# Rotary embedding by copies out of PSUM in place of a product with a permutation, and a forget gate with both weight parts in one tile, in a two-block transformer kernel on one Trainium2 core

## The chip, the cores and the metric

The kernel runs on one core of a Trainium2 chip. The metric is the device time of one launch in microseconds (us). Five engines matter: PE multiplies matrices (PEld is its weight load), DVE and ACT work elementwise, POOL does small sums, fills and a few transfers, and SP issues the large transfers. Each takes its instructions strictly in the order in which the program lists them. PE writes into PSUM, here eight banks of 128 partitions x 512 f32; DVE and ACT read it.

## The reference, cut to what matters

A sequence of 256 tokens of width 1024 goes through a first block (two mixers and a mixture of experts), then through two layers of a second block. Each of these two layers is: feed-forward, mixer, feed-forward. The change lies in the mixer alone, which therefore runs twice. There, eight "fox" heads have a forget gate, and four "diff" heads have a rotary embedding on q and k:

```
proj = h @ w_in
fq, fk, fv, ff, dq, dk, dv = jnp.split(proj, IN_OFFSETS, axis=-1)
log_f = jax.nn.log_sigmoid(ff + forget_bias);  cum_f = jnp.cumsum(log_f.transpose(0, 2, 1), axis=-1)
def _apply_rope(t, cos, sin):
    t1, t2 = jnp.split(t, 2, axis=-1)          # halves of a head of 64
    rot = jnp.concatenate([-t2, t1], axis=-1)
    return t * cos + rot * sin
```

All matrices are f32. A product is computed from parts: hi is the factor rounded for PE's fast f32r form and lo is the rest, and three products (hi hi, hi lo, lo hi) are summed in PSUM.

## The kernel before, in words

**Weights.** SP loads weights into slots. For each half of a slot (128x1024), ACT makes `whi` (L140) and DVE makes `wlo` (L154). The class Feeder holds six such pairs: a pair is refilled when PE is done with it, so `whi` waits for PE, and `wlo` waits for `whi`. The fill instructions stand in the queues of ACT and DVE among all their other work, at the place where the program called `fd.done` or `fd.tick`.

**Order in the mixer.** `feat_block` (L324) computes 512 columns of the projection, transposed (columns on partitions, tokens along the row), in two PSUM banks: eight steps of 12 matmuls each. After each step it calls `fd.tick`, which advances the background generators by one `yield`: this is what places the mixer's small work. Four PSUM buffers `g` go round, two for each block. The sequence is: dv (`skew_first`), dk, dq, fk, fq (four `feat_block`s), fv (`tok_block`), then the output product.

- `small_parts` (L1567) runs in the ticks of the dk block: `rsb` (the norm's row scales), the forget gate product `ff` (8 steps of three matmuls, L295 to L297), then the chain of small operations on `fz` and `fe` with Exp and Ln on ACT (L1581 to L1589), and last cos and sin times the row scales, `cr` and `sr` (L1594, L1595). WH and WL hold hi and lo of the gate weights in 128 columns of which 8 are used.
- `rope` (L1606) runs in the ticks of the block behind its own: for k in the dq block, for q in the fk block. ACT copies both banks to `raw` (L1610). After two ticks, for each bank b: PE multiplies `raw` by the permutation `rot` (L1616, plain f32), DVE multiplies this by `sr` (L1618) and `raw` by `cr` (L1619), and adds the two into the heads (L1627 for k, in two halves; L1630 for q).
- `diff` (L1640 on) starts when q is done: scores on PE (`ds`, L1648 and L1649), masked maximum on DVE (L1529, L1530), Exp on ACT (L1531, L1532), normalization on DVE (L1659 to L1665), transposes `t` (L1635) and the product with v (`do`). `ds` and `t` share two PSUM buffers `a`. `fox` follows in the same way.

Of the kernel before, what the change touches and what calls it, by code (L numbers as in the profile page):

```python
# [10 lines left out]
F32 = mybir.dt.float32  # L11
# [5 lines left out]
AF = mybir.ActivationFunctionType  # L17
ALU = mybir.AluOpType
# [8 lines left out]
NEG = -1e30  # L27
# [153 lines left out]
def body(tc, A, out, taps=None, stop=None):  # L181
# [3 lines left out]
    with es:  # L185
# [12 lines left out]
        def pa(name="a"):  # L198
            return psum.tile([128, 512], F32, tag="a", name=name, bufs=2)
# [7 lines left out]
        mm = nc.tensor.matmul  # L207
        act = nc.scalar.activation
        dve = nc.vector
        pool = nc.gpsimd  # L210
# [83 lines left out]
        def mm3(o, sh, sl, mh, ml, start, stop, skip=False):  # L294
            mm(o, sh, mh, start=start, stop=False, skip_group_check=skip)  # L295
            mm(o, sh, ml, start=False, stop=False, skip_group_check=skip)  # L296
            mm(o, sl, mh, start=False, stop=stop, skip_group_check=skip)  # L297
# [81 lines left out]
        XH, XL = halves(const, ("XH", "XL"))  # L379
# [97 lines left out]
        banks = feat_block()  # L477
        for h in range(4):
            z = halfbank(banks, h)
# [5 lines left out]
        banks = feat_block()  # L485
        for h in range(4):
            z = halfbank(banks, h)
# [4 lines left out]
        for i in range(2):  # L492
            c = slice(i * 512, (i + 1) * 512)
# [212 lines left out]
        banks = tok_block()  # L706
# [4 lines left out]
        banks = feat_block()  # L711
        for c in range(4):
            act(qm[:, c], halfbank(banks, c), AF.Identity, bias=qb8[:, c:c + 1], scale=-0.125)
        banks = feat_block()
        for c in range(4):
            z = halfbank(banks, c)
            act(kp[0:64, 2 * c], z[0:64], AF.Identity, bias=bcol[0:64, 20 + c:21 + c])
            act(kp[64:128, 2 * c + 1], z[64:128], AF.Identity, bias=bcol[64:128, 20 + c:21 + c])
        banks = tok_block()
# [614 lines left out]
        cos_, sin_ = aux[:, 0:256], aux[:, 256:512]  # L1334
        PTs = [aux[:, 1024 + i * 384:1408 + i * 384] for i in range(2)]
        wff = wr[:, 0:128].rearrange("p (l n) -> p l n", l=2)
        rot, tri = aux[:, 512:640], aux[:, 640:896]
        pool.dma_start(aux[:, 512:896], A["late"])

        def gain(row):  # L1340
            g = work.tile([128, 1024], F32, name="gain", bufs=1)
# [192 lines left out]
        def mixer(l, g_next):  # L1534
# [11 lines left out]
            PD = [s_p[:, i * 384:(i + 1) * 384] for i in range(5)]  # L1546
            PF = [xn[i // 2][:, (i % 2) * 384:(i % 2 + 1) * 384] for i in range(4)]
            WH = OH[:, 0:4].rearrange("p c (a n) -> p (c a) n", n=128)
            WL = OL[:, 0:4].rearrange("p c (a n) -> p (c a) n", n=128)
            wf = wff[:, l].rearrange("p (k n) -> p k n", k=8)  # L1550
            banks = [pg(), pg()]
            skew_first(banks)
            for a in (OH, OL):
                pool.memset(a[:, 0:4].bitcast(F32), 0.0)
            for a in (s_kd, s_qf, s_kf):
                pool.memset(a, 0.0)
            for a in (qf, kf):
                pool.memset(a[64:66, 0:8:2], 1.0)
                pool.memset(a[0:2, 1:8:2], 1.0)
            act(WH[:, :, 0:8], wf, AF.Copy)  # L1560
            dve.tensor_sub(WL[:, :, 0:8], wf, WH[:, :, 0:8].bitcast(F32))
            for t in range(2):
                act(vd[:, t], banks[t], AF.Copy, scale=RS[t][:, 0:1])

            def small_parts():
                yield from wait(2)
                rows = rstd_rows()  # L1567
                next(rows)
                yield from wait(3)
                for _ in rows:  # L1570
                    pass


                p = pa("ff")
                for k in range(8):
                    mm3(p[:, 0:256], WH[:, k], WL[:, k], XH[:, k], XL[:, k], k == 0, k == 7)
                    if k == 3:
                        yield
                z = work.tile([8, 256], F32, name="fz", tag="fh")
                e = work.tile([8, 256], F32, name="fe", tag="fh")  # L1580
                dve.tensor_tensor(z, p[0:8, 0:256], rsb[0:8], ALU.mult)  # L1581
                dve.tensor_scalar(z, z, fbi[:, l:l + 1], None, op0=ALU.add)
                dve.scalar_tensor_tensor(e, z, -1.0, z, op0=ALU.mult, op1=ALU.max)
                dve.tensor_scalar(z, z, 0.0, None, op0=ALU.min)
                act(e, e, AF.Exp, scale=-1.0)
                act(e, e, AF.Ln, bias=1.0)
                dve.tensor_sub(z, z, e)
                dve.tensor_tensor_scan(e, fone, z, 0.0, ALU.mult, ALU.add)
                dve.tensor_scalar(z, e, -1.0, None, op0=ALU.mult)  # L1589
                for par in range(2):  # L1590
                    r0 = 64 * (1 - par)
                    pool.dma_start(kf[r0:r0 + 1, par:8:2], e[4 * par:4 * par + 4])
                    pool.dma_start(qf[r0 + 1:r0 + 2, par:8:2], z[4 * par:4 * par + 4])
                dve.tensor_tensor(cr, cos_, rsb, ALU.mult)  # L1594
                dve.tensor_tensor(sr, sin_, rsb, ALU.mult)  # L1595

            def h2(a):
                return a.rearrange("p (h t) -> p h t", h=2)
# [7 lines left out]
            def rope(banks, scale, dst, name):  # L1606
                cb = cr[:, None, :].to_broadcast([128, 2, 256])
                sb = sr[:, None, :].to_broadcast([128, 2, 256])
                for b in range(2):
                    act(raw[:, 2 * b:2 * b + 2], h2(banks[b]), AF.Copy, scale=scale)  # L1610
                yield
                yield
                for b in range(2):
                    x2 = raw[:, 2 * b:2 * b + 2]
                    p = pa("ro")
                    mm(p, rot, x2.rearrange("p h t -> p (h t)"), start=True, stop=True)  # L1616
                    r2 = h2(rots[b])
                    dve.tensor_tensor(r2, h2(p), sb, ALU.mult)  # L1618
                    dve.tensor_tensor(x2, x2, cb, ALU.mult)  # L1619
                    dst(b, x2, r2)  # L1620
                    yield
                state[name] = True

# [225 lines left out]
def host(I):  # L1849

    I = {k: np.asarray(v) for k, v in I.items()}
    f = np.float32
    A = {}
    A["xT"] = I["x"][0].T.reshape(8, 128, S).transpose(1, 0, 2)
    A["x"] = I["x"]
    A["w_in"] = I["w_in"][0]
    A["bcol"] = np.concatenate([I["b_in"][0], I["ln1_b"][0], I["ln1_g"][0]]).reshape(60, 128).T
    A["b_in"] = I["b_in"]
    A["lbc"] = I["lb_logits"].reshape(2, 4, 128).transpose(2, 0, 1)
    for n in ("hg_norm_g", "rel_bias", "ln1_g", "ln1_b", "ln2_g", "ln2_b"):  # L1860
        A[n] = I[n]
    for n in ("w_proj_a", "w_proj_b", "w_out"):
        A[n] = I[n][0]
    for n in ("w_gate_up", "w_down"):
        A[n] = I[n][0].reshape(NE, -1, 2, 128, 1024).transpose(0, 1, 3, 2, 4).reshape(NE, -1, 128, 2048)
    c = np.zeros((128, C_END), f)
    c[:, C_ID:C_ID + 128] = np.eye(128)
    r = np.arange(128)
    c[:, C_UP:C_UP + 128] = r[:, None] < r[None, :]
    c[:, C_I:C_I + 128] = np.arange(128)  # L1870
    A["cst"] = c
    late = np.zeros((128, 384), f)
    for m in range(128):
        if m % 64 < 32:
            late[m + 32, m] = -1.0
        else:
            late[m - 32, m] = 1.0
    late[:, 256:384] = np.where(r[None, :] > r[:, None], -NEG, 0.0)
    A["late"] = late
    lv = np.zeros((128, 7, 128), f)  # L1880
    for i in range(7):
        h = 1 << i
        s_, t_ = r[:, None], r[None, :]
        lv[:, i] = (s_ // (2 * h) == t_ // (2 * h)) & (s_ % (2 * h) < h) & (t_ % (2 * h) >= h)
    A["lvl"] = lv.reshape(128, 896)
    dist = 255 - np.arange(384)
    d = np.maximum(dist, 1).astype(f)
    lp = 16 + (np.log(d / f(16)) / f(math.log(128 / 16)) * f(16)).astype(np.int32)
    bkt = np.where(dist < 16, dist, np.minimum(lp, 31))
    A["oneh"] = -((bkt[None, :] == np.arange(32)[:, None]) & (dist >= 0)[None, :]).astype(f)  # L1890
    A["mrow"] = np.broadcast_to(np.where(dist >= 0, 0.0, -NEG).astype(f), (8, 384))
    A["w_rt"] = np.concatenate([I["w_group"][0], I["w_expert"][0]], 1).reshape(8, 128, 36).transpose(1, 0, 2)
    A["b_rt"] = np.concatenate([I["b_group"][0], I["b_expert"][0]])
    A["w_ff"] = I["w_in_2"][:, :, 1536:1544].reshape(2, 8, 128, 4, 2).transpose(2, 0, 1, 4, 3).reshape(128, 2, 64)
    A["fbias"] = I["forget_bias_2"].reshape(2, 4, 2).transpose(2, 1, 0).reshape(8, 2)
    A["subln"] = I["diff_subln_2"].T
    A["lam"] = np.stack([I["lambda_q1_2"], I["lambda_k1_2"], I["lambda_q2_2"], I["lambda_k2_2"]], 1).reshape(512)
    inv = f(1.0) / (f(10000.0) ** (np.arange(0, 64, 2, dtype=f) / f(64)))
    ang = np.arange(S, dtype=f)[None, :] * inv[np.arange(128) % 32][:, None]
    A["cossin"] = np.concatenate([np.cos(ang), np.sin(ang)], 1).astype(f)  # L1900
    for n in ("1", "2"):
        w = I[f"ffn{n}_w_gate_up_2"].reshape(2, 2, 4, 128, 2, NJ, 256)
        A["gu" + n] = w.transpose(0, 5, 1, 3, 2, 4, 6).reshape(2, NJ, 2, 128, 2048)
        A["dn" + n] = I[f"ffn{n}_w_down_2"]
    for n in ("w_in_2", "w_out_2", "ffn1_norm_2", "ffn2_norm_2", "mix_norm_2", "final_norm_2"):
        A[n] = I[n]
    return {k: np.ascontiguousarray(v) for k, v in A.items()}
# [19 lines left out]
```

## Time and profile before

| what | value |
|---|---|
| time, median of three runs | 1681.79 us (1678.40, 1681.79, 1682.06) |
| time of the profiled execution | 1678.18 us |
| its span, first to last instruction | 1676.4 us |
| PE, PEld, DVE, ACT busy | 92%, 72%, 49%, 39% |
| mean granted clock of PE | 0.975 |
| the chain that ended last | PE 56%, DVE 4%, ACT 1% (the rest in lines too small to be listed) |

The two mixers lie at about 880 to 985 us and 1372 to 1478 us. The shares of busy time are means over stages with different limits: a stretch at a time has to be read. A PE record lasts until its result has left the array, so neighbouring records overlap; what a matmul costs is the distance from its start to the next one's start.

### The profile page before, as it was taken

To read this page: it belongs to the slowest core of one execution; us is meant where nothing else is said; L and a number is where in the kernel's file an instruction comes from. 1 tells how busy PE (TensorE), PEld (TensorE's weight loads), DVE (VectorE), ACT (ScalarE), POOL (GpSimd) and SP (SyncE) were. 2 spreads that over 40 slices of the span, in tenths; PEclk is the share of its full clock that TensorE was granted. 3 is DMA by queue.
4 is the path that set the end of the run, shared out by engine and by line. 5 is a ranking of instruction groups with operands and counts; after the bars stand their busy time and mean duration, and the time that the engine had idled before them with its cause. 6 is when DMAs were issued, how large, how long until landed. Compare 5 with 4: busy or idle time off the path is not lost.

```text
span 1676.4 us, 24622 instructions
## 1 busy us (share of the span) xinstructions
PE 1544.8 (92%) x10204; PEld 1209.8 (72%) x10204; DVE 813.4 (49%) x1215; ACT 650.2 (39%) x964; POOL 99.8 (6%) x144
## 2 busy tenths in 40 slices
PE   8999997877687776899999999999999999999998
PEld 7889972222122221699989879999999989889997
DVE  5875650000000000855567866555655568665554
ACT  6456420000000100644445654444544455654442
POOL 4010020000000100100002000000000030000000
PEclk9999999989998898999999999999999999999999
DMA  9657679999999999875614545555555524465510
GB/s 351 172 182 284 259 300 422 421 421 421 421 421 421 419 421 392 350 270 179 198 38 160 215 193 201 197 189 193 189 199 186 169 65 151 176 254 186 194 58 26
DMA packets 85989, 417.53 MB, mean 249 GB/s; under 512 B 7432, under 2 KB 7640, under 8 KB 50544
## 3 DMA queue, kind: packets, MB, share of 16 engines
q1 hardware_dynamic: 82688, 407.07, 64.1%
q0 software_dynamic: 2912, 7.79, 1.6%
q8 instruction: 82, 1.34, 0.3%
q10 hardware_dynamic: 272, 1.05, 0.2%
q14 instruction: 35, 0.29, 0.0%
HBM read 414.60 MB, written 1.25 MB: 248 GB/s over the span
## 4 chain that ended last, share of the span: by engine, by line
PE 56%; DVE 4%; ACT 1%; issue 0%; POOLq 0%; DVEq 0%; POOL 0%; ACTq 0%
PE g L297 9%; PE g L296 8%; PE g L295 8%; PE o L297 5%; PE o L295 5%; PE o L296 5%; PE a L296 3%; PE a L295 3%; PE a L297 3%; DVE wlo L154 1%; PE tp L1368 1%; PE ey L1105 0%; PE fo L1746 0%; PE t L1635 0%; DVE slot L1782 0%
## 5 line engine op out<-in xcount | busy, mean ns | idle before, releaser
L154 DVE TENSOR_TENSOR wlo<-slot,whi 128x1024 fp32r<-128x1024 f32 x268 | 323.3, 1223 | 196.7 <-ACT whi L140 196.5
L140 ACT ACTIVATE whi<-slot 128x1024 fp32r<-128x1024 f32 x268 | 278.3, 1057 | 217.3 <-PE o L296 67.6
L295 PE MATMUL o<-XH,whi 128*128 128x256 f32 x640 | 177.5, 277 | 0.0
L296 PE MATMUL o<-XL,whi 128*128 128x256 f32 x640 | 177.2, 277 | 0.0
L297 PE MATMUL o<-XH,wlo 128*128 128x256 f32 x640 | 177.2, 277 | 0.0
L295 PE MATMUL g<-whi,OH 128*128 128x512 f32 x416 | 165.5, 398 | 0.0
L297 PE MATMUL g<-whi,OL 128*128 128x512 f32 x416 | 164.0, 394 | 0.0
L296 PE MATMUL g<-wlo,OH 128*128 128x512 f32 x416 | 163.1, 392 | 0.0
L295 PE MATMUL a<-XH,whi 128*128 128x256 f32 x512 | 141.8, 277 | 0.0
L296 PE MATMUL a<-XL,whi 128*128 128x256 f32 x512 | 141.7, 277 | 0.0
L297 PE MATMUL a<-XH,wlo 128*128 128x256 f32 x512 | 141.6, 277 | 0.0
L1087 DVE TENSOR_TENSOR eb<-eb,eu 128x512 f32<-128x512 f32 x8 | 5.5, 687 | 265.5 <-PE eu L1083 255.8
L296 PEld LDWEIGHTS o<-XL,whi 128*128 128x128 f32 x640 | 120.4, 188 | 0.7
L295 PEld LDWEIGHTS o<-XH,whi 128*128 128x128 f32 x640 | 120.2, 188 | 0.7
L297 PEld LDWEIGHTS o<-XH,wlo 128*128 128x128 f32 x640 | 120.2, 188 | 0.0
L295 PE MATMUL g<-XH,whi 128*128 128x256 f32 x384 | 114.2, 297 | 0.0
L296 PE MATMUL g<-XL,whi 128*128 128x256 f32 x384 | 107.0, 279 | 0.0
L297 PE MATMUL g<-XH,wlo 128*128 128x256 f32 x384 | 107.0, 279 | 0.0
L1086 ACT ACTIVATE eb<-eg 128x512 f32<-128x512 f32 x8 | 4.8, 597 | 241.7 <-PE eu L1083 191.8
L296 PEld LDWEIGHTS a<-XL,whi 128*128 128x128 f32 x512 | 96.2, 188 | 0.7
L295 PEld LDWEIGHTS a<-XH,whi 128*128 128x128 f32 x512 | 96.1, 188 | 0.7
L297 PEld LDWEIGHTS a<-XH,wlo 128*128 128x128 f32 x512 | 96.2, 188 | 0.0
(531 smaller groups left out, 3486.8 us busy)
## 6 DMA issues: line engine op xcount, KB each, us to landing
slot<-in_gu_dram SPq DMA_DIRECT2D x71, 1024.0 KB, 4.9
slot<-in_w_gate_up_dram SPq DMA_DIRECT2D x46, 1024.0 KB, 19.8
slot<-in_w_in_dram SPq DMA_DIRECT2D x35, 1024.0 KB, 5.1
slot<-in_dn_dram SPq DMA_DIRECT2D x35, 1024.0 KB, 4.9
ew<-in_w_gate_up_dram SPq DMA_DIRECT2D x31, 1024.0 KB, 19.8
slot<-in_w_down_dram SPq DMA_DIRECT2D x29, 1024.0 KB, 19.8
e<-in_w_gate_up_dram SPq DMA_DIRECT2D x15, 1024.0 KB, 19.8
ew<-in_w_down_dram SPq DMA_DIRECT2D x14, 1024.0 KB, 19.8
```

Of the source, the lines that this page charges most:

```text
L140: self.nc.scalar.activation(hi[:, c], src[:, c], AF.Copy)
L154: self.low.tensor_tensor(lo[:, c], src[:, c], hi.bitcast(F32)[:, c], ALU.subtract)
L295: mm(o, sh, mh, start=start, stop=False, skip_group_check=skip)
L296: mm(o, sh, ml, start=False, stop=False, skip_group_check=skip)
L297: mm(o, sl, mh, start=False, stop=stop, skip_group_check=skip)
L1086: act(esg, g, AF.Silu)
L1087: dve.tensor_tensor(esg, esg, u, ALU.mult)
L1368: nc.tensor.transpose(p[:, i * 128:(i + 1) * 128], src[:, c], ident)
```

## The change: copies in place of the product, and both gate parts in one tile

Rotary embedding: `raw` is no longer a copy of the bank. DVE reads the bank and multiplies by the scale and by `cr` in one instruction (L1612). ACT copies the bank too, in four instructions of 32 partitions, each to the partitions of the other half of the head (L1615), so that `rots` holds the permuted values. The sign goes into the sine table. DVE then multiplies by `sr` (L1619) and adds. The product with `rot`, and `rot` itself, are gone. One bank is begun in each of the first two ticks; before, both were copied in the first.

Forget gate: lo of the gate weights goes to columns 32 to 39 of WH. One matmul with XH and one with XL for each of the eight steps give hi and lo results on different partitions; ACT copies the lo rows out (L1581), and DVE adds them (L1582).

```diff
@@ mixer @@
-            for a in (OH, OL):
-                pool.memset(a[:, 0:4].bitcast(F32), 0.0)
+            pool.memset(OH[:, 0:4].bitcast(F32), 0.0)
-            dve.tensor_sub(WL[:, :, 0:8], wf, WH[:, :, 0:8].bitcast(F32))
+            dve.tensor_sub(WH[:, :, 32:40], wf, WH[:, :, 0:8].bitcast(F32))
@@ small_parts @@
                 for k in range(8):
-                    mm3(p[:, 0:256], WH[:, k], WL[:, k], XH[:, k], XL[:, k], k == 0, k == 7)
+                    for a, x in enumerate((XH, XL)):
+                        mm(p[:, 0:256], WH[:, k], x[:, k], start=k + a == 0, stop=k + a == 8)
...
-                dve.tensor_tensor(z, p[0:8, 0:256], rsb[0:8], ALU.mult)
+                act(e, p[32:40, 0:256], AF.Copy)
+                dve.tensor_tensor(z, p[0:8, 0:256], e, ALU.add)
+                dve.tensor_tensor(z, z, rsb[0:8], ALU.mult)
@@ rope @@
                 for b in range(2):
-                    act(raw[:, 2 * b:2 * b + 2], h2(banks[b]), AF.Copy, scale=scale)
-                yield
-                yield
+                    dve.scalar_tensor_tensor(raw[:, 2 * b:2 * b + 2], h2(banks[b]), scale, cb, op0=ALU.mult, op1=ALU.mult)
+                    for r in range(0, 128, 32):
+                        act(rots[b][r:r + 32], banks[b][r ^ 32:(r ^ 32) + 32], AF.Copy, scale=scale)
+                    yield
                 for b in range(2):
-                    x2 = raw[:, 2 * b:2 * b + 2]
-                    p = pa("ro")
-                    mm(p, rot, x2.rearrange("p h t -> p (h t)"), start=True, stop=True)
                     r2 = h2(rots[b])
-                    dve.tensor_tensor(r2, h2(p), sb, ALU.mult)
-                    dve.tensor_tensor(x2, x2, cb, ALU.mult)
-                    dst(b, x2, r2)
+                    dve.tensor_tensor(r2, r2, sb, ALU.mult)
+                    dst(b, raw[:, 2 * b:2 * b + 2], r2)
                     yield
@@ tables @@
-    A["cossin"] = np.concatenate([np.cos(ang), np.sin(ang)], 1).astype(f)
+    sign = np.where(np.arange(128) % 64 < 32, f(-1.0), f(1.0))[:, None]
+    A["cossin"] = np.concatenate([np.cos(ang), sign * np.sin(ang)], 1).astype(f)
```

In the built program the order on DVE moves as follows, in the first mixer from the gate's end to q's end (`wlo` is the feeder's split, `slot_74` holds `cr`, `sr` and `rots`, `slot_76` is `raw`, `slot_69` is q):

```order
 L154 TENSOR_TENSOR wlo<-slot_71,whi 128x1024
+L1612 SCALAR_TENSOR_TENSOR slot_76<-g,slot_74 128x512 x2
 L154 TENSOR_TENSOR wlo<-slot_72,whi 128x1024
-L1618 TENSOR_TENSOR slot_74<-ro,slot_74 128x512
-L1619 TENSOR_TENSOR slot_76<-slot_76,slot_74 128x512
+L1619 TENSOR_TENSOR slot_74<-slot_74 128x512
 L1627 TENSOR_TENSOR eXL<-slot_76,slot_74 64x2x256 x2
```

The first multiplication of k now stands ahead of one `wlo`, and the second behind it; for q the same happens around the `wlo` of `slot_70`. The number of DVE instructions on the embedding is the same.

On ACT, in the same stretch, with the semaphores that each instruction waits for (before):

```order
L1586 ACTIVATE fe<-fe 8x256 [waits Activation_49]
L140 ACTIVATE whi<-slot_71 128x1024 [waits PE_49]
L1610 ACTIVATE slot_76<-g 128x512
L1610 ACTIVATE slot_76<-g 128x512 [waits PE_49]
L140 ACTIVATE whi<-slot_72 128x1024 [waits DMAHW1_49,PE_49]
```

and with the change:

```order
L1588 ACTIVATE fe<-fe 8x256 [waits Activation_49]
L140 ACTIVATE whi<-slot_71 128x1024 [waits PE_49]
L1615 ACTIVATE slot_74<-g 32x512 [waits DVE_49]
L1615 ACTIVATE slot_74<-g 32x512 x3
L140 ACTIVATE whi<-slot_72 128x1024 [waits DMAHW1_49,PE_49]
```

Two copies that waited for no engine but PE have become eight, and the first copy of each bank waits for DVE. The count of `DVE_49` that it waits for is the one that L1612 on the same bank brings about: the building layer keeps two engines that read one PSUM bank in the order of the program. The `whi` of `slot_72` stands behind the first bank's copies.

## Rows read from the trace of the kernel before

**Rows 1.** Chain that ended last, 914 to 934 us: start, us, what.

```profile
915.41 0.87 PE ro L1616 x2
...
932.04 0.49 PE ds L1648 x2
```

**Rows 2.** Windows of 10 us: us, PE, PEld, DVE, ACT, POOL busy, clock, DMA.

```profile
900.00:910.00 10.00, 10.00 (x77) 9.04 (x76) 9.77 (x13) 4.16 (x5) 1.88 (x4) 1.00 0.34 107
```

**Rows 3.** Timeline of PE in the forget gate: start, us, instruction, idle before.

```profile
894.10 0.28 PE L296 MATMUL ff<-XL,OH 128*128 128x256 f32 x1
894.22 0.28 PE L297 MATMUL ff<-XH,OL 128*128 128x256 f32 x1
```

**Rows 4.** Timeline of PE around the first product with the permutation.

```profile
900.00 1.02 PE L1616 MATMUL ro<-slot,slot 128*128 128x512 f32 x2
900.46 0.68 PE L295 MATMUL g<-XH,whi 128*128 128x256 f32 x1
900.98 0.28 PE L296 MATMUL g<-XL,whi 128*128 128x256 f32 x1
```

**Rows 5.** Timeline of DVE, gate to first scores, first mixer.

```profile
894.61 0.41 DVE L1581 TENSOR_TENSOR fz<-ff,rsb 8x256 f32<-8x256 f32 x1 [2.59 <-PE ff L297]
...
900.10 2.34 DVE L154 TENSOR_TENSOR wlo<-slot,whi 128x1024 fp32r<-128x1024 f32 x2
902.37 0.67 DVE L1618 TENSOR_TENSOR slot<-ro,slot 128x512 f32<-128x512 f32 x1
...
907.91 3.50 DVE L154 TENSOR_TENSOR wlo<-slot,whi 128x1024 fp32r<-128x1024 f32 x3
912.76 1.23 DVE L154 TENSOR_TENSOR wlo<-slot,whi 128x1024 fp32r<-128x1024 f32 x1 [1.36 <-ACT whi L140]
...
916.30 0.69 DVE L1618 TENSOR_TENSOR slot<-ro,slot 128x512 f32<-128x512 f32 x1 [0.23 <-PE ro L1616]
...
918.23 1.22 DVE L154 TENSOR_TENSOR wlo<-slot,whi 128x1024 fp32r<-128x1024 f32 x1
919.37 0.28 DVE L1529 CUSTOM_DVE_ANT_0 slot<-ds,slot 128x128 f32<-128x128 f32 x1
```

**Rows 6.** Timeline of ACT in the same stretch.

```profile
895.88 0.42 ACT L1585 ACTIVATE fe<-fe 8x256 f32<-8x256 f32 x1 [3.54 <-DVE fe L1583]
...
898.88 1.05 ACT L1610 ACTIVATE slot<-g 128x512 f32<-128x512 f32 x2
899.84 1.04 ACT L140 ACTIVATE whi<-slot 128x1024 fp32r<-128x1024 f32 x1
```

**Rows 7.** Groups of ACT instructions by form: count, busy us, mean ns, idle before.

```profile
L736 ACT ACTIVATE g<-g,bcol 128x256 f32<-128x256 f32 x16 | 6.2, 470 | 0.0
L1678 ACT ACTIVATE junk<-do 128x128 bf16<-128x128 f32 x16 | 4.4, 273 | 1.8 <-PE do L1671 1.3
L1610 ACT ACTIVATE slot<-g 128x512 f32<-128x512 f32 x8 | 4.2, 577 | 0.0
L718 ACT ACTIVATE slot<-g,bcol 64x256 f32<-64x256 f32 x4 | 1.9, 469 | 0.1
```

**Rows 8.** Groups of DVE instructions by form.

```profile
L1782 DVE SCALAR_TENSOR_TENSOR slot<-g,rsb 64x512 f32<-64x512 f32 x12 | 8.2, 687 | 0.2
```

**Rows 9.** Timeline of PE at the first scores and at the second transposes.

```profile
917.52 0.39 PE L1648 MATMUL ds<-eXL,slot 128*128 128x128 f32 x2
...
931.09 0.83 PE L1635 MATMUL t<-cst,slot 128*128 128x128 f32 x3 [0.17 <-DVE slot L1665]
932.04 0.49 PE L1648 MATMUL ds<-eXL,slot 128*128 128x128 f32 x2
```

**Rows 10.** Windows of 1 us of PE in the experts' stage: us, busy, clock, DMA.

```profile
657.00:658.00 1.00, 0.70 (x7) 1.00 1.01 414
660.00:661.00 1.00, 0.00 (x0) 0.50 1.01 397
663.00:664.00 1.00, 1.00 (x8) 0.50 1.03 410
666.00:667.00 1.00, 1.00 (x12) 0.69 0.84 328
```

More of the change, by code (lines that the diff above doesn't have):

```diff
@@ L1336, in body @@
         wff = wr[:, 0:128].rearrange("p (l n) -> p l n", l=2)
-        rot, tri = aux[:, 512:640], aux[:, 640:896]
-        pool.dma_start(aux[:, 512:896], A["late"])
+        tri = aux[:, 640:896]
+        pool.dma_start(tri, A["late"])
         def gain(row):
@@ L1548, in mixer @@
             WH = OH[:, 0:4].rearrange("p c (a n) -> p (c a) n", n=128)
-            WL = OL[:, 0:4].rearrange("p c (a n) -> p (c a) n", n=128)
             wf = wff[:, l].rearrange("p (k n) -> p k n", k=8)
@@ L1871, in host @@
     A["cst"] = c
[L1872 to L1878, printed above, removed]
+    late = np.zeros((128, 256), f)
+    late[:, 128:256] = np.where(r[None, :] > r[:, None], -NEG, 0.0)
     A["late"] = late
```

## The prediction, made before the changed kernel ran

> **What bounds the kernel now.** I read the page first: PE is busy 92% of the span, so what PE no longer does should be gained wherever PE is the limit. Whether it is the limit in the mixer was the second question, and three views answer it. The windows show DVE at 9.77 of 10 us between 900 and 910 us [rows 2]. The chain that ended last runs over PE up to the end of the fourth product with the permutation, at 915.41 + 0.87 = 916.28, and from there mostly over DVE (and ACT, which feeds it) until PE's `ds` at 932.04 [rows 1]: here PE has no slack of its own to give. DVE's timeline gives the reason: after the gate's chain DVE works without a pause from 900.10 to 911.4, idles 1.36 us for a `whi` and 0.23 us for the permutation, and has its last q operation done at about 918.3 [rows 5]. So the mixer's embedding is a race: PE needs q at its first score, 917.52 [rows 9], and DVE has the first half of q ready just ahead of the 916.30 at which it begins the second, little more than 1.2 us earlier. From 932 on PE leads the chain again, so what has shifted there stays shifted to the end. The second mixer repeats the same pattern 492 us later with the same waits; I count everything twice.
>
> **What PE loses of its work.** Gate: one of three matmuls falls away in eight steps; a step in the row of `ff` is 894.22 - 894.10 = 0.12 us [rows 3], so 8 x 0.12 = 0.96 us. Permutation: from the start of `ro` to the second matmul behind it are 0.98 us, of which one ordinary matmul is 0.12, so one product costs 0.86 us [rows 4]; four of them are 3.44 us. PE thus comes to its first score 4.4 us earlier, at 917.52 - 4.4 = 913.1.
>
> **The gate's chain.** It gains nothing. `ff` ends 0.96 us earlier, but ACT now copies the lo rows (0.42 us, the price of the `fe` operation of the same 8x256 form [rows 6]) and DVE has one more operation (L1581's 0.41, with its distance to the next about 0.45 [rows 5]): 0.96 - 0.42 - 0.45 = 0.1 gained, less a handover between engines. The table load for Exp now stands behind that copy, but ACT idled 3.54 us before Exp [rows 6] and it still fits. Bounds: 0.1 us gained to 0.3 lost. I take 0: `cr` and `sr` are ready at 900.1 as before.
>
> **The embedding on DVE and ACT.** The price of one ACT copy is unknown in its form (32x512 out of PSUM). ACT's price does not follow the partitions: 64x256 takes 469 ns, 128x256 takes 470 [rows 7]. The old copy of 128x512 took 577 ns by itself, and two in a row took 899.84 - 898.88 = 0.96 us, 0.48 each [rows 6, 7]. I take 0.48; as bounds 0.27 (the 128x128 out of PSUM) and 0.577 [rows 7]. DVE's operations keep their number and price: L1612 takes the place of L1619, and the same form from PSUM costs 687 ns [rows 8], 0.65 from start to start.
>
> What decides is a new wait. ACT's first copy of a bank waits until L1612 on that bank is done, and the `whi` behind the four copies stands in front of the `wlo` that DVE meets after its two L1612. Step by step from 900.10, with `wlo` at 1.17 apiece (2.34 for two, 3.50 for three [rows 5]):
>
> - k: `wlo` to 901.25; L1612 twice, done at 901.9 and 902.5. ACT copies bank 0 from 901.95, 4 x 0.48 = 1.9, then `whi` 1.04 [rows 6]: 904.9. DVE, free at 902.5, has `wlo` next and idles 2.4 us. Then `wlo` to 906.1 and the other six k operations. All eight took 907.91 - 902.37 = 5.54 us [rows 5]; without two at 0.65 this is 4.24, so 910.35. Bank 1's copies are over at 906.9, ahead of their need at 908.2.
> - q: three `wlo`, 3.50: 913.85. L1612 twice: 914.5, 915.1. Copies from 914.5, `whi` until 917.5; DVE idles 2.4 us again. Then `wlo` to 918.7, the first half of q at 920.05, the second at 921.4.
>
> Before, the `wlo` behind q started at 918.23 [rows 5]; now it starts at 921.3. This is 3.1 us later, and the sum agrees: 2 x 2.4 idle added, 1.36 + 0.23 idle removed, 0.1 of rounding. In the queue behind the waiting `wlo` stand q itself, then the masked maxima, for which ACT's Exp and PE's transposes wait. DVE and ACT hand on to each other without slack from 919.37 until the chain returns to PE at 932.04, so 3.1 us is what DVE brings to that point.
>
> On PE: the first score waits for the first half of q and starts at 920.1 in place of 917.52, 2.6 us late, after 920.1 - 913.1 = 7.0 us of nothing. The 4.4 us that PE saves lie wholly in this hole.
>
> Here a rule of the Trainium skill bears. No stretch shown above has ACT and DVE reading one bank side by side: the old `raw` copies had their bank to themselves. PSUM — Partial Sum Buffer, section "PSUM bank collisions raise a hardware error", says that any two engines on one bank and the same 32 partitions collide, reads against reads included, and must be held apart by a semaphore. By it the wait is needed and the sum stands as it is; without it, the first rival's sum would hold. No run here shows a collision.
>
> **The clock.** A hole of 7 us is not free. PE stood still from about 657.7 to 663 us; the granted clock was 0.50 (1.2 GHz) by the row of 660, PE worked again from 663, and the clock returned within the row of 666 (0.69 on average, so at about 666.6) [rows 10]: some 3.6 us of work at half speed, an estimate from these rows. In the mixer this would cost PE 1.75 us behind the first score, from 0 (clock stays) to 1.8. PE has something to set against it: at the second transposes it stood waiting, 0.17 us ahead of them and then until the scores, for 932.04 - 931.09 = 0.95 us is 0.59 more than three matmuls of 0.12 [rows 9]; 0.76 in all. So PE arrives at 932's place 2.6 + 1.75 - 0.76 = 3.6 us late with the drop in full, and DVE brings 3.1 without it.
>
> **Sum.** I take 3.4 us per mixer, between these two and nearer to the drop, 6.8 in all. Against the profiled execution's own 1678.18 us (span 1676.4 and 1.8 around it) this is 1685.0. The median of the three runs is 3.6 us above that execution, and one run lies beside it; with 6.8 on the median it is 1688.6. I put the forecast between the two, at 1687.
>
> The POOL fill and the permutation's part of the table's transfer that fall away are worth 0: POOL's four forget-gate transfers and everything on it here wait for DVE's chain, and PE's third block finds its banks free (bank 1's copies end at 906.9, PE reaches it at 906.8).
>
> **The rivals.**
>
> 1. *The copies hide.* If ACT read beside L1612, it would copy bank 0 from 899.0, each `whi` would be in time, and DVE would run from 900.10 without a pause: the 1.36 and 0.23 go, q ends about 1.7 us earlier, and PE's 4.4 us saved are cut to that by the same chain. Two mixers: 3.4 us faster, 1674.8 by the profiled execution, 1678.4 by the median. For it: ACT is idle enough. Against it: the wait stands in the built order. It decides from the point where the `whi` is done before DVE has finished L1612. Chance 0.09. (All of PE's 8.8 us would need a DVE that does not bind; against this speaks 9.77 of 10 [rows 2]. It is within this chance.)
> 2. *Cheap copies.* At 0.27 us, four take 1.1, DVE idles 1.55 twice in place of 2.4, and 3.1 - 1.59 = 1.5 us per mixer are lost: 3 us in all, 1681.2 to 1684.8. For it only a form of a quarter of the row. Chance 0.13.
> 3. *The clock costs more.* If the drop lasts into the next scores, PE's lateness and DVE's add up (DVE waits for scores, PE for the maxima), to 4.5 us per mixer; with copies at 0.577 DVE's idle is 2.8 twice, 4.0 per mixer. 8 to 9 us, up to 1691. For it: two engines that hand each score back and forth. Chance 0.20.
>
> The forecast's own case (6.2 to 7.5 us) has 0.58.
>
> **How the numbers follow.** No change, which a measurement of this kernel tells to about 0.2% or 3.4 us: most of rival 2, 0.11. Faster: rival 1, 0.09. Slower: the rest, 0.80. The range goes from 1680 (rival 2 on a low run) to 1692 (rival 3 on the median); outside are rival 1 and some of the ends.
>
> **What would show it.** In the changed profile: DVE idle about 2.4 us before one `wlo` between L1612 and L1619, for ACT `whi`, in both embeddings of both mixers; L1615 near 0.48 us from start to start; PE idle about 7 us before the first `ds` with DVE named; a clock of 0.50 behind it; no wait between the gate's end and `sr` that is longer than before. I am wrong if DVE's `wlo` meets a finished `whi`, or if PE's hole is under 4 us.

## The result, and the profile after

| | before | after |
|---|---|---|
| time, median of four runs | 1680.53 us (1678.40 to 1682.06) | 1692.67 us (1690.42 to 1695.11) |
| ratio to before | | 1.0069, 95% interval 1.0055 to 1.0083 |
| profiled execution: time, span | 1678.18, 1676.4 us | 1690.71, 1688.9 us |
| mean granted clock of PE | 0.975 | 0.964 |
| ACT busy | 650.2 us | 666.3 us |

The change makes the kernel 0.7% (11.6 us) slower. The sign and the new wait came as forecast; the size did not: 6.8 us were expected, and the time lies just above the range.

The loss lies in a short stretch of the two mixers. A mark in front of it is the last `wlo` ahead of the gate's chain, one behind it the first normalization of head scores (L1659). These are DVE's timelines, of the kernel before and of the changed one (start, us, instruction, idle before it and what ended it):

```profile
890.80 1.23 DVE L154 TENSOR_TENSOR wlo<-slot,whi 128x1024 fp32r<-128x1024 f32 x1 [1.43 <-ACT whi L140]
...
920.41 0.29 DVE L1529 CUSTOM_DVE_ANT_0 slot<-ds,slot 128x128 f32<-128x128 f32 x1 [0.40 <-PE ds L1649]
...
921.67 1.23 DVE L154 TENSOR_TENSOR wlo<-slot,whi 128x1024 fp32r<-128x1024 f32 x1 [0.62 <-ACT whi L140]
...
923.37 0.17 DVE L1659 RECIPROCAL md<-md 128x4 f32<-128x4 f32 x1
```

```profile
890.72 1.23 DVE L154 TENSOR_TENSOR wlo<-slot,whi 128x1024 fp32r<-128x1024 f32 x1 [1.43 <-ACT whi L140]
...
898.25 0.68 DVE L1590 TENSOR_TENSOR_SCAN fe<-slot,fz 8x256 f32<-8x256 f32 x1
...
899.84 1.21 DVE L154 TENSOR_TENSOR wlo<-slot,whi 128x1024 fp32r<-128x1024 f32 x1
900.98 1.27 DVE L1612 SCALAR_TENSOR_TENSOR slot<-g,slot 128x512 f32<-128x512 f32 x2
905.23 1.23 DVE L154 TENSOR_TENSOR wlo<-slot,whi 128x1024 fp32r<-128x1024 f32 x1 [2.98 <-ACT whi L140]
...
918.46 1.23 DVE L154 TENSOR_TENSOR wlo<-slot,whi 128x1024 fp32r<-128x1024 f32 x1 [3.04 <-ACT whi L140]
...
922.26 1.22 DVE L154 TENSOR_TENSOR wlo<-slot,whi 128x1024 fp32r<-128x1024 f32 x1
923.39 0.28 DVE L1529 CUSTOM_DVE_ANT_0 slot<-ds,slot 128x128 f32<-128x128 f32 x1
...
926.61 0.29 DVE L1529 CUSTOM_DVE_ANT_0 slot<-ds,slot 128x128 f32<-128x128 f32 x1 [2.58 <-PE ds L1649]
...
929.28 0.17 DVE L1659 RECIPROCAL md<-md 128x4 f32<-128x4 f32 x1
```

From mark to mark it was 923.37 - 890.80 = 32.57 us and is 38.56, 5.99 more; in the second mixer 32.56 and 38.30, 5.74 more. Together 11.73 us, beside 11.6 by the ratio (9 to 14 by its interval) and the 12.5 by which the two profiled spans differ: by the spans 0.8 us is left for other places. The rows say where it is. From the mark to DVE's first masked maximum (L1529) it was 28.57 (919.37 [rows 5]) and is 32.67, 4.10 more: DVE stands for 2.98 and 3.04 us where it stood for 1.36 and 0.23 [rows 5]. From there to the normalization it was 4.00 and is 5.89, 1.89 more (1.64 in the second mixer): DVE now stands for 2.58 us in front of the second score, where it stood for 0.40, and the 0.62 for a `whi` behind it are gone.

ACT in the same stretch (answers to [rows 6]), and its copies as a group (to [rows 7]: count, busy us, mean ns, idle before):

```profile
901.68 2.43 ACT L1615 ACTIVATE slot<-g 32x512 f32<-32x512 f32 x4 [2.96 <-DVE slot L1612]
904.14 1.06 ACT L140 ACTIVATE whi<-slot 128x1024 fp32r<-128x1024 f32 x1
905.22 2.43 ACT L1615 ACTIVATE slot<-g 32x512 f32<-32x512 f32 x4
```

```profile
L1615 ACT ACTIVATE slot<-g 32x512 f32<-32x512 f32 x16 | 9.4, 589 | 7.6 <-DVE slot L1612 7.2
```

From the first copy to the `whi` behind the fourth are 904.14 - 901.68 = 2.46 us, 0.615 a copy, in place of the 0.48 assumed. ACT had been idle for 2.96 us ahead of them.

PE: rows of its timeline, the chain that ended last (answers to [rows 1, 9]), and windows of 1 us (us, PE, PEld, DVE, ACT, POOL busy, clock, DMA share, GB/s).

```profile
907.70 0.39 PE L295 MATMUL g<-XH,whi 128*128 128x256 f32 x1 [0.82 <-ACT slot L1615]
...
925.09 0.63 PE L1648 MATMUL ds<-eXL,slot 128*128 128x128 f32 x2
```

```profile
914.11 7.00 issue
921.11 0.77 PE ds L1648 x2
...
937.97 0.49 PE ds L1648 x2
```

```profile
915.00:916.00 1.00, 0.00 (x0) 0.00 (x0) 0.42 (x1) 0.97 (x2) 0.00 (x0) 1.00 1.06 414
916.00:917.00 1.00, 0.00 (x0) 0.00 (x0) 0.00 (x0) 0.95 (x3) 0.00 (x0) 0.64 1.07 414
...
922.00:923.00 1.00, 1.00 (x5) 0.82 (x5) 1.00 (x2) 1.00 (x1) 0.00 (x0) 0.50 0.06 16
...
926.00:927.00 1.00, 1.00 (x7) 0.91 (x6) 0.39 (x3) 0.23 (x2) 0.00 (x0) 0.74 1.04 430
927.00:928.00 1.00, 1.00 (x11) 1.00 (x10) 1.00 (x3) 0.95 (x4) 0.00 (x0) 1.00 0.74 303
```

The hole is 7.00 us, as forecast. The clock falls to 0.50 (1.2 GHz) inside it and returns within the row of 926 (0.74 on average, so at about 926.5), so PE works for some 5.4 us at half speed, an estimate from these rows; in the second mixer it is 5.0. The second score starts 925.09 - 921.11 = 3.98 us behind the first; before, it was 919.55 - 917.52 [rows 9] = 2.03. The place that was at 932.04 [rows 9] is at 937.97.

### The profile page after: what moved, and what is told of

Same layout as the page of the kernel before. It is cut to its first block, busy times and chain, and to the rows that moved or that the text cites. A ratio compares the mean times of both kernels' runs of the same rounds, so it can differ in the third digit from the quotient of the medians.

```text
span 1688.9 us, 24585 instructions
## 1 busy us (share of the span) xinstructions
PE 1546.9 (92%) x10172; PEld 1211.4 (72%) x10172; DVE 812.6 (48%) x1217; ACT 666.3 (39%) x990; POOL 98.4 (6%) x142
## 4 chain that ended last, share of the span: by engine, by line
PE 61%; DMA 24%; DVE 5%; issue 2%; ACT 1%; POOL 0%; POOLq 0%; DVEq 0%; SPq 0%; ACTq 0%
PE g L295 9%; PE g L297 9%; PE g L296 9%; DMA ew<-in_w_gate_up_dram 6%; DMA slot<-in_w_gate_up_dram 6%; PE o L297 5%; PE o L296 5%; PE o L295 5%; DMA slot<-in_w_down_dram 5%; PE a L296 4%; PE a L295 4%; PE a L297 4%; DMA e<-in_w_gate_up_dram 2%; DMA m<-in_w_gate_up_dram 1%; DMA ew<-in_w_down_dram 1%
```

## The experiments

The profiled executions differ by up to 5.5 us at the end of the experts' stage already, which the edits do not touch, so each kernel is compared by its measured ratio and by the two marks (interval in both mixers, less 32.57 and 32.56). Mark 1 to maximum shows DVE's delay, maximum to mark 2 what the clock adds to it; before it was 28.57 and 4.00.

| kernel | ratio, 95% interval | mark to maximum | maximum to mark 2 (both mixers) | sum against before |
|---|---|---|---|---|
| changed | 1.0069, 1.0055 to 1.0083 | 32.67 | 5.89, 5.63 | +11.7 us |
| gate alone | 0.9991, 0.9982 to 1.0000 | 28.16 | 3.99, 4.00 | -0.8 |
| embedding alone | 1.0068, 1.0054 to 1.0081 | 32.84 | 5.04, 5.20 | +10.8 |
| PE kept busy | 1.0054, 1.0040 to 1.0068 | 32.68 | 3.99, 3.99 | +8.2 |
| bank 0's copies first, k alone | 1.0035, 1.0022 to 1.0048 | 29.72 | 5.88, 5.84 | +6.0 |
| copies behind `whi` | 1.0026, 1.0016 to 1.0035 | 29.60 | 4.00, 4.59 | +2.7 |
| bank 0's copies first | 0.9981, 0.9972 to 0.9989 | 26.78 | 4.00, 4.71 | -2.9 |
| the same, sine product early | 0.9979, 0.9970 to 0.9988 | 26.78 | 4.00, 3.99 | -3.6 |
| the same, k's sums on POOL | 0.9985, 0.9975 to 0.9994 | 27.93 | 4.00, 4.00 | -1.3 |
| the same, k's sine products too | 0.9994, 0.9985 to 1.0003 | 28.32 | 3.99, 3.98 | -0.6 |
| before, k's sums on POOL | 1.0009, 1.0000 to 1.0018 | 28.64 | 4.00, 4.00 | +0.5 |

(The maximum's column is that of the first mixer; the second agrees within 0.03 us but for the last row, 28.99.)

**The gate alone.** The edit is the gate's half of the diff, put into the kernel before.

> The gate's part alone, the embedding as before. Theory (what the gate saves on PE goes into DVE's chain, and the chain's end moves by 0.1 to 0.2 us): 0 to 0.4 us faster than the kernel before, ratio 0.9997 to 1.0000; DVE's `sr` ends 0.1 to 0.3 us earlier, and PE stands about 1 us longer in front of its first score. Rival (PE's 0.96 us count in each mixer): 1.9 us faster, ratio 0.9989. Second rival (the gate's new operations are part of the loss): 1 us or more slower.

By the marks 0.4 us less per mixer, of which 0.18 lie in the gate's chain itself and 0.25 in DVE's wait for a `whi` (1.11 us in place of 1.36). This stands between the theory's 0.1 to 0.2 and the rival's 0.96; the ratio's interval excludes neither. The second rival is out: the gate is no part of the loss.

**The embedding alone.** The other half, with the gate as before.

> The embedding's part alone, the gate as before. Theory (the loss is all the embedding's: DVE idles twice about 3.0 us for a `whi` behind four copies, and PE's half clock adds to it): 11 to 12.5 us slower than the kernel before, ratio 1.0065 to 1.0075, with a hole of about 6 us in front of PE's first score in place of 7.0. Rival (the gate's PE time lengthens the hole and so the loss): 9 us or less, ratio 1.0054 or less.

The ratio is as the theory says (by the marks a little less, 10.8), but the hole is 7.00 us here too. PE stands nowhere for bank 1's copies here, for which it stood 0.82 us in the changed kernel (907.70): most of what the gate saves PE (0.96) had gone into that wait. The two parts do not add: -0.8 and +10.8 make 10.0, together they cost 11.7. In the maximum's column the difference is 0.24 per mixer; the larger part is in the clock's column, 5.04 and 5.20 against 5.89 and 5.63. In this kernel the clock was back some 3.7 and 4.0 us behind the first score, in the changed one 5.4 and 5.0 (estimates from windows of 1 us). The holes are alike; why the clock stayed low for longer in one is open.

**Bank 0's copies first.**

```diff
-  dve.scalar_tensor_tensor(raw[:, 2*b:2*b+2], h2(banks[b]), scale, cb, ...)
+  if b: times_cos()
   for r in range(0, 128, 32):
       act(rots[b][r:r+32], banks[b][r ^ 32:(r ^ 32)+32], AF.Copy, scale=scale)
+  if not b: times_cos()
```

> The changed kernel, but in each embedding ACT copies bank 0 before DVE multiplies it by the cosine (bank 1 as in the changed kernel). ACT, which idled 2.96 and 4.28 us in front of these copies, can begin them early; the `whi` behind them no longer waits for DVE. Theory (the loss comes from `whi` queued behind copies that wait for DVE, and the clock's part hangs on the hole that this makes): DVE's idle of 2.98 us in k goes, that of 3.04 us in q falls to 1.7 or less (DVE now waits there for the copies), the hole in front of PE's first score falls from 7.0 to 2 to 4 us; against the kernel before between 3 us faster and 1 us slower, ratio 0.9982 to 1.0006. Rival (the copies themselves, eight times 0.61 us of ACT in each embedding, set the time wherever they stand): 5 us or more slower, ratio 1.003 or more.

No instruction is added or taken away, and 14.6 us go (11.7 more than before, now 2.9 less). ACT, DVE and PE of this kernel:

```profile
899.78 2.41 ACT L1618 ACTIVATE slot<-g 32x512 f32<-32x512 f32 x4
902.22 1.06 ACT L140 ACTIVATE whi<-slot 128x1024 fp32r<-128x1024 f32 x1
```

```profile
902.23 1.29 DVE L1613 SCALAR_TENSOR_TENSOR slot<-g,slot 128x512 f32<-128x512 f32 x2
903.43 1.22 DVE L154 TENSOR_TENSOR wlo<-slot,whi 128x1024 fp32r<-128x1024 f32 x1
...
912.35 1.28 DVE L1613 SCALAR_TENSOR_TENSOR slot<-g,slot 128x512 f32<-128x512 f32 x2
913.55 1.22 DVE L154 TENSOR_TENSOR wlo<-slot,whi 128x1024 fp32r<-128x1024 f32 x1
```

```profile
916.19 0.46 PE L1653 MATMUL ds<-eXL,slot 128*128 128x128 f32 x2 [1.79 <-issue]
```

The copies fill time in which ACT stood still, `whi` is done when DVE asks for it, and both idle times of DVE are gone (the theory had left up to 1.7 us of the second). DVE starts on bank 0 at 902.23, behind the last of its copies: the two engines still take the bank one after the other, in the other order. The copies are as dear as in the changed kernel, so their sum is not what costs. The hole in front of the first score is 1.79 us in both mixers, yet the clock fell in the second alone (0.50 in the window of 1409), which cost 0.7 us there. This version beats both kernels.

**PE kept busy in the hole.**

```diff
   o = [po("do") for _ in range(2)]
+  for i in range(50):
+      mm(o[0][:, 0:256], XH[:, 0, 0:128], XH[:, 1], start=True, stop=True)
```

> The changed kernel with 50 more matmuls of 128x256 ahead of PE's first score in each mixer, into a bank that the output product of the heads overwrites later; they need nothing that is late. At 0.12 us each they fill 6 of the 7.0 us in which PE stood still. Theory (1.9 us of each mixer's 5.9 come from PE at half clock behind the hole, which makes DVE wait 2.58 us for the second score): the granted clock stays at 1.0 behind the hole, that wait falls under 0.5 us, and the time falls by 3 to 4 us against the changed kernel: 7.5 to 8.5 us slower than before, ratio 1.0045 to 1.005. Rival (the whole loss is DVE's own delay): no change against the changed kernel, ratio 1.007.

PE's row with the added matmuls, the first score behind them, DVE's two first maxima, and a window behind the hole:

```profile
917.29 6.16 PE L1644 MATMUL do<-XH 128*128 128x256 f32 x50
924.46 0.46 PE L1650 MATMUL ds<-eXL,slot 128*128 128x128 f32 x2 [1.01 <-issue]
```

```profile
926.74 0.28 DVE L1529 CUSTOM_DVE_ANT_0 slot<-ds,slot 128x128 f32<-128x128 f32 x1
...
927.46 0.29 DVE L1529 CUSTOM_DVE_ANT_0 slot<-ds,slot 128x128 f32<-128x128 f32 x1
```

```profile
926.00:927.00 1.00, 1.00 (x10) 1.00 (x9) 1.00 (x4) 0.61 (x1) 0.00 (x0) 1.00 0.00 0
```

The clock stays at 1.00, DVE's wait for the second score is gone, and the 1.89 and 1.64 us of the clock go; DVE's 4.1 us stay. Work that nobody needs made the kernel 3.5 us faster than the changed one by the marks (2.5 by the two ratios, whose intervals overlap). The ratio, 1.0054, stands a little above the 1.0045 to 1.005 expected.

**Both cosine products first, all copies behind `whi`.**

```diff
+  times_cos(0); times_cos(1)
+  yield
+  copies(0); copies(1)
+  yield
```

> The changed kernel with both of DVE's cosine products in the first tick and all eight of ACT's copies in the second, so that `whi` stands in front of the copies and not behind four of them; no instruction is added or taken away. Theory (what costs is `whi` queued behind the copies): DVE's `wlo` finds its `whi` done, DVE waits for the copies instead, about 1.2 and 0.4 us in k, 1.2 and 1.1 us in q, so 2 us less in each mixer: 5 to 8 us slower than before, ratio 1.003 to 1.005. Rival (the eight copies of 0.61 us decide, wherever they stand): ratio 1.006 to 1.008, as the changed kernel.

Better than the theory's figure: the waits for copies were 0.77 and 0.27 us in k, 0.83 and 1.03 in q. The eight copies stand there as before; only what is queued behind them has changed. The clock fell in both mixers, behind holes of 3.66 and 3.88 us; in the first this added nothing (4.00), in the second 0.6 us. DVE begins its maxima 3.4 us behind the first score here (925.38 - 921.98), against 2.28 in the changed kernel, and in the first mixer the clock was back 3.3 us behind that score, in the second only 5.0 (estimates from windows of 1 us).

**Bank 0's copies first for k alone.**

> The changed kernel with bank 0's copies first for k alone; q as in the changed kernel. Theory (the two idle times of DVE add up): the 2.98 us in k go and the 3.04 us in q stay, the hole in front of PE's first score is 4 us with a granted clock that still falls behind it, and the time is 3 us lower in each mixer: 4 to 6.5 us slower than before, ratio 1.0025 to 1.004. Rival (the second idle time takes in the first, since q waits for its own copies anyway): 9 us or more slower, ratio 1.0055 or more.

```profile
918.79 1.23 DVE L154 TENSOR_TENSOR wlo<-slot,whi 128x1024 fp32r<-128x1024 f32 x1 [3.04 <-ACT whi L140]
...
926.94 0.29 DVE L1529 CUSTOM_DVE_ANT_0 slot<-ds,slot 128x128 f32<-128x128 f32 x1 [2.58 <-PE ds L1654]
```

k's 2.95 us are gone from the maximum's column, q's idle time and the clock's cost are as they were, behind a hole of 4.91 us. The two idle times add up, as the prediction had it.

**The sine product of bank 0 early.** On top of the copies first, DVE does L1619 and the sum of bank 0 before the `wlo` of the second tick.

> As the kernel in which ACT copies bank 0 first, and DVE does the sine product and the sum of bank 0 already in the second tick, ahead of the `wlo` (1.17 us) that stood before them; the ticks in all, and so PE's order, are unchanged. Theory (in that kernel DVE works without a pause from the gate to the scores, so PE waits for a total that no order shortens): PE's hole of 1.8 us in front of the first score falls to about 0.6, but the masked maxima start at the same time, and the time changes by 0 to 1 us each mixer: ratio to the kernel before 0.997 to 0.9985. Rival (what PE waits in front of the first score counts by itself): 1.2 us or more each mixer, ratio 0.9965 or less.

PE's hole is 0.66 us, the maxima start at the same 26.78, and the second mixer's clock no longer falls. The ratio can't be told from that of the kernel it builds on. So the theory holds: up to the maxima DVE's work is the limit, not the hole by itself.

**The price of a copy, in two kernels.** They change only the form of the copies.

> The changed kernel with other forms of the four copies, for their price alone: for k each of the four copies the whole bank (128x512), for q each copies its 32 partitions without moving them; the output is not rotary embedding. Theory (the price is that of the 512 elements in the row and of the instruction, and the old pair's 0.48 us came from the two of them overlapping): 0.6 us from start to start in all forms, DVE's idle 3.0 us in both embeddings. Rival (moving to other partitions costs): q's copies at 0.48 us, DVE's idle there 2.5 us. Second rival (a row of 32 partitions costs more than one of 128): k's at 0.48 us and k's idle 2.5.

> The changed kernel with other forms of the copies once more, for their price alone: for k four copies of a whole bank (128x512) in turn to two tiles, so that no copy writes where the one before it wrote; for q two copies of 64 partitions each, unmoved; the output is not rotary embedding. Theory (copies of all 128 partitions that depend on nothing before them overlap by 0.1 us, those of a part of the partitions run strictly one after the other): k's 0.48 us from start to start, q's 0.60 us each, so DVE idles 2.4 us in k and 1.7 to 1.9 us in q. Rival (0.6 us is what any copy of 512 elements out of PSUM takes when several read one bank): k's at 0.6 us, DVE's idle there 2.9 us.

ACT's timeline of the first (k: the whole bank four times into one tile; q: 32 partitions, unmoved) and of the second (k: the whole bank, in turn into two tiles; q: 64 partitions):

```profile
907.71 2.48 ACT L1616 ACTIVATE slot<-g 128x512 f32<-128x512 f32 x4 [2.96 <-DVE slot L1612]
910.09 1.05 ACT L140 ACTIVATE whi<-slot 128x1024 fp32r<-128x1024 f32 x1
...
920.79 2.38 ACT L1618 ACTIVATE slot<-g 32x512 f32<-32x512 f32 x4 [4.43 <-DVE slot L1612]
923.20 1.06 ACT L140 ACTIVATE whi<-slot 128x1024 fp32r<-128x1024 f32 x1
```

```profile
907.08 2.06 ACT L1616 ACTIVATE slot<-g 128x512 f32<-128x512 f32 x4 [2.96 <-DVE slot L1612]
909.00 1.08 ACT L140 ACTIVATE whi<-slot 128x1024 fp32r<-128x1024 f32 x1
...
920.14 1.19 ACT L1619 ACTIVATE slot<-g 64x512 f32<-64x512 f32 x2 [5.26 <-DVE slot L1612]
921.35 1.06 ACT L140 ACTIVATE whi<-slot 128x1024 fp32r<-128x1024 f32 x1
```

From start to start: 0.63 us for whole banks that each write over the one before (a record is 0.60, so the fourth starts at 907.71 + 2.48 - 0.60 = 909.59, three distances behind the first); 0.60 for 32 and 0.605 for 64 partitions; 0.48 for whole banks that do not write over the one just before. Of the copies only these overlap one another: each record is 0.60 us long, and the next starts 0.48 behind its start. With them DVE's idle time in k was 2.47 us, the forecast's 2.4. The first kernel's theory (0.6 in all forms) did not tell these apart; the second's does.

**k's sums on POOL.** DVE is the limit, so it was relieved of four sums (4 x 0.69 us), then of two sine products too; and the kernel before got the same sums as a control.

```diff
-  dve.tensor_tensor(kd[pr_, 4*b+c:4*b+4:2], x2[pr_], r2[pr_], ALU.add)
+  pool.tensor_tensor(kd[pr_, 4*b+c:4*b+4:2], x2[pr_], r2[pr_], ALU.add)
```

> As the kernel with bank 0's copies and its sine product early, and k's four sums (64x512, 0.69 us apiece on DVE) go from DVE to POOL, where 128x512 sums took 1.28 us. Theory (with the waits gone DVE's work is the limit up to the scores, and what PE saves is gained only as DVE is relieved): 2.1 to 2.8 us less in each mixer, ratio to the kernel before 0.9945 to 0.9955. Rival (PE's order or POOL's slower sums set the time): ratio 0.9975 to 0.9985, as without it.

> The same, with k's two sine products on POOL too (two more operations of 0.68 us leave DVE). Theory: another 0 to 1.3 us less in each mixer, since PE comes to its first score with no more than 0.7 us to spare and becomes the limit; ratio to the kernel before 0.992 to 0.9955. Rival (POOL, now with some 7.7 us of k's work, ends behind q): slower than with the sums alone.

> The kernel before with nothing changed but k's four sums on POOL: how much of a gain of those sums is due to the change. Theory (here PE is at its first score without a pause, and DVE could be earlier by 1.2 us at most before it waits for that score): 0 to 1.2 us less in each mixer, ratio 0.9985 to 1.0. Rival (relieving DVE is worth the same in both kernels): ratio 0.9965 or less.

The theory fell: none of the three gains by it. DVE and POOL with the sums alone:

```profile
906.91 0.95 DVE L1620 TENSOR_TENSOR slot<-slot 128x512 f32<-128x512 f32 x1 [0.74 <-ACT slot L1616]
908.00 6.58 DVE L154 TENSOR_TENSOR wlo<-slot,whi 128x1024 fp32r<-128x1024 f32 x3
```

```profile
905.17 8.32 POOL L1638 TENSOR_TENSOR eXL<-slot,slot 64x512 f32<-64x512 f32 x4 [1.45 <-DVE slot L1620]
```

Three `wlo`, 3.50 us otherwise [rows 5], take 6.58 beside POOL's sums, and a sum takes 2.08 us. DVE loses 3.1 us for the 2.8 that it was spared, and having less to do it now stands 0.74 us for bank 1's copies. The control shows the same slowness (6.77 us for its three `wlo`). The Trainium skill, SBUF — State Buffer, section "SBUF: two separate sides", names a port pair that DVE and POOL hold one at a time, for a whole instruction, where DVE reads two inputs from SBUF and POOL reads SBUF; these rows agree in that both engines become slower.

The kernel with the sine products on POOL too says one thing more, on the clock (rows of PE, of DVE, and a window):

```profile
919.48 0.46 PE L1659 MATMUL ds<-eXL,slot 128*128 128x128 f32 x2 [2.19 <-issue]
```

```profile
923.08 0.28 DVE L1529 CUSTOM_DVE_ANT_0 slot<-ds,slot 128x128 f32<-128x128 f32 x1
```

```profile
921.00:922.00 1.00, 1.00 (x7) 1.00 (x6) 0.97 (x3) 0.98 (x2) 0.00 (x0) 0.50 0.00 0
```

Behind holes of 2.19 and 2.15 us the clock fell to 0.50 in both mixers, and yet from the maximum to mark 2 it is 3.99 and 3.98, as without a drop. DVE begins its maxima 923.08 - 919.48 = 3.60 us behind the first score, and stands 0.33 us for the second, against 0.40 before the change: the scores' lead covers the whole drop.

## Why the prediction was right, and where it was wrong

- **What bounds the stretch: right.** DVE's chain does. PE's saved 4.4 us are gained in no version. The best gains 1.79 us per mixer, which is DVE's former idle time and the gate's part: 1.36 + 0.23 + 0.2. This is close to the first rival's sum (1.7 per mixer, 3.4 in all; by the marks 3.6).
- **The new wait: right, in place and kind.** `whi` queued behind four copies that wait for DVE stops DVE in both embeddings. Taking the order apart takes the loss away. The two engines' turns at a bank were needed in some order, not in this one: with ACT first they still take turns, and the first rival's sum comes out all the same.
- **The copy's price: wrong, and outside its bounds.** "I take 0.48", bounded by 0.577. Measured 0.615. The 0.48 was the spacing of two whole-bank copies, which overlap; copies of a part of the partitions run strictly one after the other. That "ACT's price does not follow the partitions" holds for the duration of one, not for the next one's start. Four copies are 0.54 us longer, so each idle time is 3.0 and not 2.4: 1.1 to 1.2 us per mixer. The `wlo` behind q started at 922.26, not at 921.3.
- **The gate's chain: nearly right.** 0.2 us gained where I took 0.
- **The hole: right.** 7.0 us, each end 1.0 us later than forecast; PE's third block did wait for bank 1's copies, 0.82 us, which I had put at 0.
- **The clock: the step that failed most.** "So PE arrives at 932's place 2.6 + 1.75 - 0.76 = 3.6 us late with the drop in full, and DVE brings 3.1 without it", and then "I take 3.4 us per mixer, between these two". This treats the two delays as alternatives of which the later counts. It rests on "DVE and ACT hand on to each other without slack from 919.37", and that was misread: DVE stood 0.40 us there for PE's second score (920.41, above), so PE was in that loop already. The delays follow one another: DVE, late by 4.1, finishes q; only then does PE compute the scores, at half clock, and DVE waits for the second one. The drop cost 1.64 to 1.89 us per mixer, near the 1.75 estimated for PE, but on top of DVE's delay, and the 0.76 of PE's earlier waits set nothing against it. Mixer by mixer 4.1 + 1.89 and 4.1 + 1.64, 11.7 in all against 6.8: of the 2.5 us per mixer that were missing, 1.0 is DVE's (the copies' 1.2 less the gate's 0.2) and 1.5 the clock's.
- **The rivals.** The third described this sum (4.5 per mixer, though its own terms, 3.1 and 1.75, make 4.9), and the dearer copies (4.0), but each for itself; both came together.

## What to carry to other kernels

Where an engine is given work that waits for another, look first at what is queued behind it in its own queue; the same work put where the engine stands still can turn a loss into a gain. A delay of one engine and a clock drop of another can add up when the two hand work back and forth: here they did, by 1.0 to 1.9 us, where DVE's maxima began 2.3 us behind the first score, and not at all in three of four mixers where they began 3.4 to 3.6 us behind it. Take a price from a pair of instructions only for a form that overlaps in the same way.

## What the runs showed of the hardware that was not expected

- ACT copies out of PSUM, 512 f32 in a row: 0.48 us from start to start where all 128 partitions are copied and none writes over the one just before; 0.60 to 0.615 for 32 or 64 partitions, and 0.63 where each writes over the one before. The Trainium skill, ScalarE: Activation LUTs, section "What ACT_TABLE_LOAD costs", gives an overlap of about 93 ns for instructions back to back; the first form agrees (0.58 us of duration, 0.48 of spacing), the others do not have it.
- DVE operations with two inputs in SBUF took 1.9 times as long beside POOL's sums (6.58 us for 3.50).
- PE's clock fell to 0.50 behind holes of 7.00, 4.91, 3.66 and 2.19 us in front of the first score, in both mixers each time; behind 1.79 us it fell in one mixer and not in the other, and it did not fall behind 1.87 (k's sums on POOL) and 0.66 us.
